# A transformer layer's modulation rows on six tiles, gates loaded a step ahead, and a staging tile in another pool

## The chip, the cores and the metric

The kernel runs on one core of a Trainium2 chip. The metric is device time in microseconds (us) of one execution. "Before" is the median of three runs: 2761.38 us (2759.38 to 2765.55). The profile is of one further execution.

Names of the engines in the profile: PE is TensorE (matrix products and transposes), PEld its weight load, DVE is VectorE, ACT is ScalarE, POOL is GpSimd, SP is SyncE, which here issues most of the transfers. Each engine takes its instructions in the order of its own queue. SPq and POOLq are the queues from which SyncE and GpSimd issue transfers.

## What is computed

One layer of a diffusion backbone on 256 latent tokens `x` and 256 context tokens `ctx`, width D = 2048, all in float32. Each sub-layer is normalised and modulated by rows of a product of a condition vector with `w_mod`; nine such rows (`N_MOD`) belong to each of the two sequences.

```python
def adaln(x, g, mod, i):
    return rms_norm(x, g) * (1 + mod[:, i + 1, None, :]) + mod[:, i, None, :]

def half_step_ffn(x, mod, i, g, w_up, w_down):
    h = adaln(x, g, mod, i)
    a, b = jnp.split(h @ w_up, 2, axis=-1)
    return x + 0.5 * mod[:, i + 2, None, :] * ((jax.nn.silu(a) * b) @ w_down)

def reference(...):
    mod_l = (silu_c @ w_mod[l] + b_mod[l]).reshape(B, N_MOD, D_MODEL)
    mod_c = (silu_cc @ w_mod[l] + b_mod[l]).reshape(1, N_MOD, D_MODEL)
    xl = half_step_ffn(xl, mod_l, 0, g_norm[l, 0], w_ffn1_up[l], w_ffn1_down[l])
    xc = half_step_ffn(xc, mod_c, 0, g_norm[l, 0], w_ffn1_up[l], w_ffn1_down[l])
    hl = adaln(xl, g_norm[l, 1], mod_l, 3)
    hc = adaln(xc, g_norm[l, 1], mod_c, 3)
    ...
    (aq_l, ak_l, av_l), m_l = mixer_projections(hl, *mix, rope)
    (aq_c, ak_c, av_c), m_c = mixer_projections(hc, *mix, None)
    hm_c, st_f, st_b = mlstm_bidir(*m_c[:3], *m_c[4:], zero_state, zero_state)
    hm_l, _, _ = mlstm_bidir(*m_l[:3], *m_l[4:], st_f, st_b)
    att_l = latent_attention(aq_l, ...)
    xl = xl + mod_l[:, 5, None, :] * mixer_output(att_l, hm_l, m_l[3], m_gain[l], w_out[l])
    xl = half_step_ffn(xl, mod_l, 6, g_norm[l, 2], w_ffn2_up[l], w_ffn2_down[l])
    return rms_norm(xl, g_final)
```

The mixer has 8 attention heads and 8 mLSTM heads of width 128. An mLSTM head takes query and key through a short convolution (5 taps) and Silu.

## The kernel before, in words

**Products.** A float32 weight tile of 128 x 2048 arrives in `raw` (three buffers) or `chain_` (two). `split` makes of each half `hi` (ScalarE, L102: a rounding copy) and `lo` (VectorE, L103: what the rounding left). `mm3` (L124 to L126) then multiplies three times: high by high, high by low, low by high. TensorE so needs both engines for each tile, `lo` last. `hi` and `lo` have four buffers each.

**Order of the stages.** FFN1's up projection runs in groups of products (`quad`), then its down projection in pairs of blocks (`pair`), a single last block (`last1`), the mixer's projections `w_c`, `w_a`, `w_b` (with gate algebra for the mLSTM, `gate_steps`), `w_mk` (eight heads), `w_mq` (eight heads), attention, `w_out`, and FFN2. By the matmuls of the profile `last1` begins near 1380 us, `w_c` 1427, `w_a` 1456, `w_b` 1492, `w_mk` 1540, `w_mq` 1645; attention and the heads' outputs go on to about 1892.

**Modulation beside the products.** One half-row block of `w_mod` (512 KB) is loaded into a tile `sraw` and multiplied by the broadcast condition `cBl` and summed by one VectorE instruction (`mod_half`, L183), pinned in program order. In the mixer `mod_late` hands 96 such items (rows 5 to 7) to `mod_items`, a generator stored in `beside["part"]`. `products_of` and `channels` take one step of it every few matmuls. `pace` maps items to steps: an item comes once `done` has reached the interpolated step. Two tiles serve all items: after each item the next but one is asked for into the tile that was just read, so SyncE's queue (L212) stands until VectorE has read it. `conditions` loads the other half of `cBl` when the items pass to the second half. `mod_end` finishes a row, `mod_rows_out` turns and stores it.

**Down projection.** `pair(p)` goes through seven products per pair of blocks, each for two column halves `c`. `chain_` is updated in place by accumulating transfers on GpSimd (`accum`). In the last pair the sums pass through the gate (`through_gate`, L853), and `both_gates` loads (L858) the gate rows of both sequences to 128 partitions (256 KB each) into a two-buffer tile `gate`, in the step that uses them. `last1` loads one gate half per column block in the same manner and writes through a one-buffer tile `y`.

**Hidden tiles.** FFN1's hidden state passes over HBM: `turned` transposes a tile, ScalarE copies it to `stg`, and SyncE stores it to `hidd` (profile: `hid<-stg`). `stg` lies in pool `f1u`. When that pool closes, pool `f1` with `acc` and the two-buffer tiles `two` (here named `v` and `gate`) takes its space. `last_steps` asks for two hidden tiles of the last block at step 8 of the last quad, on which two products of the first pair depend.

**mLSTM.** `conv` (L1175 on VectorE) and Silu lead to `mkT` and `mqT`. `state` (L1188, tile `vw`) makes the context's final state, two steps per head. `latents` loads `nM` for a head, multiplies key with query (L1241), makes the decay matrix `E` (L1250 on VectorE, L1252 and L1253 Exp on ScalarE, a mask on GpSimd), and `heads_out` ends with `hm` (L1293, L1294). Exp and Silu need different activation tables; ScalarE loads one at each change.

Pool `m1` holds most of this. `one(...)` makes a tile of one buffer; a `tag` names the slot it lives in, so that tiles with one tag share the space one after the other.

Of the kernel before, what the change touches and what calls it, by code (L numbers as in the profile page):

```python
# [18 lines left out]
P = 128  # L19
# [29 lines left out]
def tile_layer(ctx: ExitStack, tc: tile.TileContext, I: dict, out: bass.AP):  # L49
# [106 lines left out]
    class Conditions:  # L156


        def __init__(self, half, load, at):
            self.half, self.load, self.at = half, load, at  # L160
# [81 lines left out]
    def mod_late(sp, i0, i1, pace):  # L242

        cB = sp.tile([P, 1024], F32, name="cBl", bufs=1)
        cond = Conditions(lambda h: h, lambda h: conditions({LAT: cB}, h, h + 1, (LAT,)), lambda h: {LAT: cB})
        raws = lambda: sp.tile([P, 1024], F32, tag="sraw", name="sraw", bufs=2)
        return mod_items(half_items(i0, i1), nc.sync.dma_start, raws, 2, cond, None, pace)

    def mod_end(i, seqs):

# [322 lines left out]
    with pool(name="f1u", bufs=1) as f1u:  # L573
# [87 lines left out]
        def turned():  # L661

            if not turn:
                return
            n, t, ca = turn.pop(0)
            tb = tbank()
            for j in range(FB):
                nc.tensor.transpose(tb[:, j * P : (j + 1) * P], ca[:, j * P : (j + 1) * P], ident)
            stg = f1u.tile([P, CB], F32, tag="stg", name="stg")
            nc.scalar.activation(stg, tb, AF.Copy, scale=-1.0)  # L670
            nc.sync.dma_start(hidd[n][:, t].rearrange("p j c -> p (j c)"), stg)

# [102 lines left out]
        def last_steps(step):  # L775

            steps(side)
            if step == 8:
                raws.extend(hid_slot("n"))
                for m in range(2):  # L780
                    hid_load(m, raws[m].bitcast(F32))
            if step == 10:
                place0.extend(x.rearrange("p (a c) -> p a c", a=2) for x in hid_slot("s"))
            if step in (11, 12):
                split_to(place0[step - 11], quarters(raws[step - 11].bitcast(F32))[0])
# [69 lines left out]
    def both_gates(cb, seqs=(CTX, LAT)):  # L855
        g = two("gate")
        for s in seqs:
            nc.sync.dma_start(g[:, s, :], mod_rows[2][s, cb * CB : (cb + 1) * CB].partition_broadcast(P))  # L858
        return g

    NP = (NB - 1) // 2

    def pair(p):

        X, Y, Z, ra, gates = {}, {}, {}, {}, None
        w = lambda m, cb: I["w_dn1"][2 * p + m, cb]

        def put(t, cb, b, first=False):
            if first and p == 0:
                nc.scalar.activation(col(t, cb), b, AF.Copy)  # L870
            else:
                nc.vector.tensor_tensor(col(t, cb), col(t, cb), b, op=ALU.add)

        def through_gate(t, cb):

            if p < NP - 1:
                return
            s, tt = divmod(t, 2)
            half_gated(col(t, cb), col(t, cb), gates[:, s, :], -1.0 if cb % 2 else 1.0)
            accum(col(t, cb), xsrc[s][tt * P : (tt + 1) * P, cb * CB : (cb + 1) * CB])  # L880

        def c11x(c, s):
            put(2 * s, 2 * c, X[c, s], True)

        def c11z(c, s):
            put(2 * s, 2 * c, Z[c, s])
            through_gate(2 * s, 2 * c)

        def p5(c, s):
            put(2 * s + 1, 2 * c + 1, Y[c, s], True)  # L890

        def p35(c, s):
            put(2 * s, 2 * c + 1, Y[c, s], True)

        def c12(c, s):
            put(2 * s, 2 * c + 1, X[c, s])
            through_gate(2 * s, 2 * c + 1)

        def x3(c, s):
            put(2 * s + 1, 2 * c, X[c, s], True)  # L900
            put(2 * s + 1, 2 * c + 1, X[c, s])
            through_gate(2 * s + 1, 2 * c + 1)

        def c21(c, s):
            put(2 * s + 1, 2 * c, Y[c, s])
            through_gate(2 * s + 1, 2 * c)

        def loaded(m, cb):
            raw = raw_tile()
            nc.sync.dma_start(raw, w(m, cb))  # L910
            return raw

        def again(c):
            if p + 1 < NP:
                nc.sync.dma_start(chain_[c], I["w_dn1"][2 * p + 2, 2 * c])

        def b22(c):
            ra[c] = loaded(1, 2 * c + 1)
            return ra[c]

        held = lambda c: chain_[c]

        order = (
            ("a11", held, X, True, lambda c: accum(chain_[c], w(0, 2 * c + 1)), c11x, None),
            ("a12", lambda c: loaded(1, 2 * c), Z, True, None, c11z, 0),
            ("n1", held, Y, True, lambda c: accum(chain_[c], w(1, 2 * c + 1)), p5, None),
            ("s4", b22, Y, False, lambda c: accum(ra[c], w(0, 2 * c + 1)), p35, None),
            ("s2", held, X, False, lambda c: accum(chain_[c], w(1, 2 * c)), c12, 1),
            ("s3", lambda c: ra[c], X, False, None, x3, 1),
            ("a22", held, Y, True, again, c21, 0),  # L930
        )
        todo = first_plan if p == 0 else plan if p < NP - 1 else last_plan
        for m, (g, src, dst, fresh, then, use, gate) in enumerate(order):
            a = place0[m] if p == 0 and m < 2 else place[g]
            for c in range(2):
                wt = split(src(c))
                if then:
                    then(c)
                for x in todo.get(2 * m + c, "").split():
                    if x.startswith("raw"):  # L940
                        hid_load(2 * p + 2 + int(x[3]), raws[int(x[3])])
                    else:
                        make[x]()
                if p == NP - 1 and gate is not None:
                    gates = both_gates(2 * c + gate)
                for s in range(2):
                    if fresh:
                        dst[c, s] = tbank() if c and dst is not X else bank()
                    for j in range(FB):
                        k = slice((FB * s + j) * P, (FB * s + j + 1) * P)  # L950
                        mm3(dst[c, s], a[:, 0, k], a[:, 1, k], *wt(slice(j * CB, (j + 1) * CB)), fresh and j == 0, j == FB - 1, True)
                    use(c, s)
# [20 lines left out]
    def last1():  # L973

        norm = iter(())
        kept = {}
        for s in (CTX, LAT):
            for n, cb in enumerate((1, 3, 0, 2) if s == CTX else (2, 0, 3, 1)):
                c = slice(cb * CB, (cb + 1) * CB)
                wt = kept.pop(cb, None) or load_split(I["w_dn1"][NB - 1, cb])  # L980
                if s == CTX and n >= NCB - 2:
                    kept[cb] = wt
                g = both_gates(cb, (s,))[:, s, :]
                for t in range(2 * s, 2 * s + 2):
                    b = bank()
                    block_products(b, wt, t)
                    a = acc[:, t, c]
                    y = f1.tile([P, CB], F32, tag="xr", name="y", bufs=1)
                    half_gated(y, b, g)
                    nc.vector.tensor_tensor(a, a, y, op=ALU.add)  # L990
                    if s == LAT:
                        nc.sync.dma_start(x1d[(t - 2) * P : (t - 1) * P, c], a)
                    if n == 0:
                        ss1[t] = sm.tile([P, 4], F32, tag="ss4", name="ss4", bufs=4)
                    sumsq(ss1[t][:, cb : cb + 1], a)
                    steps(norm, (1, 0, 0, 0, 2, 2, 2, 2)[2 * n + t % 2])
            drain(norm)
            norm = adaln(s)
        return norm
# [32 lines left out]
    with ExitStack() as mx:  # L1032
# [21 lines left out]

        mmcm = pool(name="mm", bufs=1)

        beside["part"] = mod_late(mmcm.__enter__(), 5, 8, ((45, 44), (75, 96), (96, 160)))
        ev_mv(6, 0, b_c)
        b_a = {}
        drain(project("w_a", 416, range(4), b_a))  # L1060
# [13 lines left out]
        def gates():  # L1074
# [35 lines left out]
            for d in range(2):  # L1110
# [15 lines left out]
                nc.vector.tensor_tensor_scan(Mq, uq, uq, m3, ALU.max, ALU.max)  # L1126
                nc.vector.tensor_copy(hc[:, d, 4 + a : 5 + a], m2)
                nc.vector.tensor_tensor(hc[:, d, 4 + z : 5 + z], m2, btT[:, d, 2 + a : 3 + a], op=ALU.add)
            negM = one([NH, 2, T], "negM")
            nc.vector.tensor_scalar(negM, MT.rearrange("h d t q -> h d (t q)"), -1.0, None, op0=ALU.mult)  # L1130
            nc.sync.dma_start(negMd, negM)

# [26 lines left out]


        mkT = one([P, NH, T], "mkT")
        mqT = one([P, NH, T], "mqT")
        C1 = one([P, NH, 2, 130], "C1")

        def conv(b, ch, ns):
# [12 lines left out]
        def state(h, kTc):  # L1178
# [3 lines left out]
                nc.tensor.transpose(tb[:, t * P : (t + 1) * P], kTc[:, t * P : (t + 1) * P], ident)  # L1182
            kn = m1.tile([P, 2, P], F32, tag="kn", name="kn", bufs=1)
            nc.scalar.activation(kn, tb[:, :256].rearrange("p (t d) -> p t d", t=2), AF.Copy)
            vw = m1.tile([P, 2, 2, 130], F32, tag="vw", name="vw", bufs=1)
            for t in range(2):
                for d in range(2):
                    nc.vector.tensor_scalar(vw[:, t, d, :], v1[CTX][:, t, h, :], wg[:, t, d, h : h + 1], None, op0=ALU.mult)  # L1188
# [36 lines left out]
            todo.append((h, y))  # L1225


        hm = one([P, 2, 1024], "hm")
        ready = [0]

# [551 lines left out]
```

## Time and profile before

| what | us |
|---|---|
| median of the runs | 2761.38 |
| profiled execution | 2753.58 |
| its span | 2751.9 |
| TensorE clock granted over the span, of full | 0.986 |
| `L183` in the mixer: 96 instructions | 116.6 |
| `L103` lo, 128x1024, in 1440 to 1900: 76 instructions | 94.2 |

The profile gives busy times per engine, waits by engine, line and releaser (us in total, times, longest), and windows, which give each engine's busy time in a stretch with the granted clock and the transfer share. One group row reads: line, engine, operation, tiles out and in, number; busy time and mean in ns; idle time ahead of it and who ended it. For the modulation in the mixer, 1440 to 1900 us, that group is:

```profile
L183 DVE SCALAR_TENSOR_TENSOR sraw<-sraw,cBl 128x1024 f32<-128x1024 f32 x96 | 116.6, 1221 | 44.9 <-DMA sraw<-in_w_mt 42.0 <-DMA cBl<-ccd 2.4
```

The last figures say that VectorE stood idle for 44.9 us ahead of these 96 instructions, 42.0 of them until a row had landed. All 224 such loads of the kernel, of 512 KB each, take a median of 5.3 us from issue to landing:

```profile
sraw<-in_w_mt SPq DMA_DIRECT2D x224, 512.0 KB, 5.3
```

### The profile page before, as it was taken

Reading aid. Unit: us, or ns where it says so; the run is one execution under the profiler, and the core shown is the slowest. Engines: PE = TensorE matmul, PEld = TensorE weight load, DVE = VectorE, ACT = ScalarE, POOL = GpSimd, SP = SyncE. Lnnn points to the kernel's source line nnn. Section 1 sums busy time; section 2 is a strip of 40 time slices with the busy share of each in tenths; the row PEclk is TensorE's granted clock in tenths of the full one; section 3 lists DMA queues with packets and bytes.
Section 4 is the critical chain, followed back from the end, with each engine's and each line's share of the span. In section 5 each row is a group of like instructions: output and inputs, shape, how many; then the busy total and the mean of one; then the engine's idle time right before and its main releaser. Section 6 shows DMA issues by size and latency. Waiting matters only on the chain. (4 is left out here: it accounts for less than half of the span.)

```text
span 2751.9 us, 33080 instructions
## 1 busy us (share of the span) xinstructions
PE 2647.2 (96%) x12573; PEld 2180.0 (79%) x12573; DVE 1995.5 (73%) x2740; ACT 1263.4 (46%) x1586; POOL 174.6 (6%) x217
## 2 busy tenths in 40 slices
PE   6999999999999889999999998999999999999998
PEld 3588878887878768888789788877898888888886
DVE  2387778778877778888786789797685666666657
ACT  3454444544444455444363335345474444444444
POOL 0000000110000000000210000111000000000000
PEclk8999999999999999999999999999999999999999
DMA  8879999999999969889966766574466666666553
GB/s 349 313 233 249 246 274 277 263 269 268 269 254 266 269 193 239 224 233 219 227 220 217 257 236 234 178 259 161 163 230 227 216 228 223 217 225 225 211 190 132
DMA packets 125887, 645.32 MB, mean 235 GB/s; under 512 B 13464, under 2 KB 17560, under 8 KB 68256
## 3 DMA queue, kind: packets, MB, share of 16 engines
q1 hardware_dynamic: 106144, 513.18, 51.7%
q0 software_dynamic: 19584, 130.03, 24.1%
q8 instruction: 99, 1.62, 0.2%
q14 instruction: 60, 0.49, 0.0%
HBM read 627.36 MB, written 15.79 MB: 234 GB/s over the span
## 5 line engine op out<-in xcount | busy, mean ns | idle before, releaser
L103 DVE TENSOR_TENSOR lo<-raw,hi 128x1024 fp32r<-128x1024 f32 (+3 forms) x600 | 720.3, 1205 | 399.7 <-ACT hi L102 388.4
L102 ACT ACTIVATE hi<-raw 128x1024 fp32r<-128x1024 f32 (+3 forms) x600 | 625.2, 1045 | 796.4 <-PE mm L126 644.5
L125 PE MATMUL mm<-lo,hhi 128*128 128x512 f32 (+3 forms) x1024 | 392.5, 383 | 15.1 <-DVE lo L103 15.0
L124 PE MATMUL mm<-hi,hhi 128*128 128x512 f32 (+3 forms) x1024 | 394.2, 388 | 4.4 <-ACT v L1053 4.4
L126 PE MATMUL mm<-hi,hlo 128*128 128x512 f32 (+3 forms) x1024 | 391.0, 382 | 0.0
L102 ACT ACTIVATE hi<-chain 128x1024 fp32r<-128x1024 f32 x240 | 251.8, 1058 | 264.7 <-PE mm L126 129.5
L103 DVE TENSOR_TENSOR lo<-chain,hi 128x1024 fp32r<-128x1024 f32 x240 | 289.3, 1220 | 98.0 <-ACT hi L102 96.5
L183 DVE SCALAR_TENSOR_TENSOR c<-sraw,cBh 128x1024 bf16<-128x1024 f32 x192 | 229.3, 1218 | 36.8 <-DMA sraw<-in_w_mt 33.5
L124 PE MATMUL mm<-hi,h2hi 128*128 128x512 f32 x640 | 249.1, 389 | 0.0
L125 PE MATMUL mm<-lo,h2hi 128*128 128x512 f32 x640 | 249.0, 389 | 0.0
L126 PE MATMUL mm<-hi,h2lo 128*128 128x512 f32 x640 | 249.0, 389 | 0.0
L125 PEld LDWEIGHTS mm<-lo,hhi 128*128 128x128 f32 x1024 | 195.8, 191 | 51.3 <-DVE lo L103 19.8
L124 PEld LDWEIGHTS mm<-hi,hhi 128*128 128x128 f32 x1024 | 194.5, 190 | 36.6 <-ACT v L1053 4.8
L126 PEld LDWEIGHTS mm<-hi,hlo 128*128 128x128 f32 x1024 | 195.3, 191 | 34.0
L183 DVE SCALAR_TENSOR_TENSOR sraw<-sraw,cBl 128x1024 f32<-128x1024 f32 x128 | 155.6, 1220 | 44.9 <-DMA sraw<-in_w_mt 42.0
L124 PE MATMUL mm<-hhi,hi 128*128 128x512 f32 (+1 forms) x384 | 142.0, 371 | 1.2 <-ACT hi L102 1.2
L124 PEld LDWEIGHTS mm<-hi,h2hi 128*128 128x128 f32 x640 | 120.1, 188 | 25.2
L125 PEld LDWEIGHTS mm<-lo,h2hi 128*128 128x128 f32 x640 | 120.1, 188 | 24.8
L126 PEld LDWEIGHTS mm<-hi,h2lo 128*128 128x128 f32 x640 | 120.1, 188 | 24.8
L126 PE MATMUL mm<-hhi,lo 128*128 128x512 f32 (+1 forms) x384 | 137.9, 361 | 1.2 <-DVE lo L103 1.2
L124 PE MATMUL mm<-hi,hid2h 128*128 128x512 f32 x352 | 138.5, 395 | 0.0
L125 PE MATMUL mm<-hlo,hi 128*128 128x512 f32 (+1 forms) x384 | 138.4, 361 | 0.0
(377 smaller groups left out, 4719.3 us busy)
## 6 DMA issues: line engine op xcount, KB each, us to landing
sraw<-in_w_mt SPq DMA_DIRECT2D x224, 512.0 KB, 5.3
raw<-in_w_up2b SPq DMA_DIRECT2D x80, 1024.0 KB, 4.7
raw<-in_w_dn SPq DMA_DIRECT2D x70, 1024.0 KB, 4.8
chain<-in_w_up1b POOLq DMA_DIRECT2D x60, 1024.0 KB, 11.0
raw<-in_w_up1b SPq DMA_DIRECT2D x40, 1024.0 KB, 8.8
mraw<-in_w_m SPq DMA_DIRECT2D x32, 1024.0 KB, 8.0
chain<-in_w_dn POOLq DMA_DIRECT2D x30, 1024.0 KB, 9.3
chain<-in_w_up1b SPq DMA_DIRECT2D x20, 1024.0 KB, 7.1
```

The lines of the kernel that those rows point to most:

```text
L102: nc.scalar.activation(hi, src, AF.Copy)
L103: nc.vector.tensor_tensor(lo, src, hi.bitcast(F32), op=ALU.subtract)
L124: nc.tensor.matmul(out_ap, sh, mh, start=first, stop=False, skip_group_check=skip)
L125: nc.tensor.matmul(out_ap, sh, ml, start=False, stop=False, skip_group_check=skip)
L126: nc.tensor.matmul(out_ap, sl, mh, start=False, stop=last, skip_group_check=skip)
L183: ins = nc.vector.scalar_tensor_tensor(junk() if junk else raw, raw, 1.0, cB[s], op0=ALU.mult, op1=ALU.mult, accum_out=mT[:, i, s, kt, h : ...
```

## The change

Three things are changed.

*Modulation in the mixer.* The class `Beside` takes the place of `mod_late` there (FFN2 keeps the old one). It has six tiles: three `sr` of its own in pool `mm`, two halves of a tile in the slot of `mqT`, one in the slot of `rt`; both slots are used for their own tiles only later. The first six loads are issued by GpSimd, the others by SyncE. The next load into a tile is issued when one further step has passed since its use (`due`). The three borrowed tiles serve the first 50 items; `close_early` ends that before `mqT` is made, ahead of the w_mq heads. The pace is new. To make room, `negM` shares the slots `nM`, and `vw` the slots `E`, in place of slots of their own.

*Gates of the down projection.* In the last pair the table `GATES` says at which half-step which column block's gates are loaded; `ahead` holds those not used yet, and `s3` uses the gates that `s2` used. `last1` has a ring of four half tiles, each loaded two blocks ahead.

*Staging tile.* `stg` and `last1`'s `y` lie in pool `chp`, which lasts to the end of the down projection. The hidden tiles of the last block are asked for at step 6 of the last quad and not 8.

```diff
+    class Beside:
+        def __init__(self, sp, i0, i1, early, n_early, pace):
+            self.cB = sp.tile([P, 1024], F32, name="cBl", bufs=1)
+            self.items = half_items(i0, i1)
+            self.n_early, self.pace = n_early, pace
+            self.slots = {}
+            self.n = self.done = self.waits = self.asked = 0
+            self.due, self.late = [], []
+            for x in [sp.tile([P, 1024], F32, name=f"sr{j}", bufs=1) for j in range(3)]:
+                self.fetch(x, False, nc.gpsimd)
+            for x in early:
+                self.fetch(x, True, nc.gpsimd)
+
+        def fetch(self, x, early, queue):
+            if self.asked >= (self.n_early if early else len(self.items)):
+                return
+            i, kt, h = self.items[self.asked]
+            pin(queue.dma_start(x, I["w_mt"][i - 2, kt, :, h * 1024 : (h + 1) * 1024]))
+            self.slots[self.asked] = x, early
+            self.asked += 1
+
+        def one(self):
+            i, kt, h = self.items[self.n]
+            x, early = self.slots[self.n]
+            mod_half(x, {LAT: self.cB}, None, i, (LAT,), kt, h)
+            self.due.append((self.done + 1, self.n))
+            self.n += 1
+
+        def finish(self, n):
+            i, kt, h = self.items[n]
+            x, early = self.slots.pop(n)
+            self.fetch(x, early, nc.sync)
+            left[i] -= 1
+            if not left[i]:
+                self.late += [(self.done + 2, i, s, v) for s, v in mod_end(i, (LAT,))]
+
+        def close_early(self):
+            while self.n < self.n_early:
+                self.one()
+            while self.due:
+                self.finish(*self.due.pop(0)[1:])
+
+        def steps(self):
+            half = None
+            while self.n < len(self.items) or self.due or self.late:
+                while self.n < len(self.items):
+                    h = self.items[self.n][2]
+                    if h != half:
+                        half = h
+                        conditions({LAT: self.cB}, h, h + 1, (LAT,))
+                        self.waits += WAIT
+                    if self.done < np.interp(self.n, *zip((0, 0), *self.pace)) + self.waits:
+                        break
+                    self.one()
+                yield
+                self.done += 1
+                for x in [x for x in self.due if x[0] <= self.done]:
+                    self.due.remove(x)
+                    self.finish(*x[1:])
+                if self.late and self.late[0][0] <= self.done:
+                    mod_rows_out(*self.late.pop(0)[1:])
...
-            stg = f1u.tile([P, CB], F32, tag="stg", name="stg")
+            stg = chp.tile([P, CB], F32, tag="stg", name="stg")
...
-            if step == 8:
+            if step == 6:
                 raws.extend(hid_slot("n"))
...
+    LAST = [(CTX, cb) for cb in (1, 3, 0, 2)] + [(LAT, cb) for cb in (2, 0, 3, 1)]
+    last_gates = []
+
+    def last_gate(i):
+        if i % 4 in (0, 2) and len(last_gates) < 4:
+            g = two("gate")
+            last_gates.extend((g[:, 0, :], g[:, 1, :]))
+        if i < len(LAST):
+            s, cb = LAST[i]
+            nc.sync.dma_start(last_gates[i % 4], mod_rows[2][s, cb * CB : (cb + 1) * CB].partition_broadcast(P))
...
+        GATES = {0: 0, 1: 2, 4: 1, 5: 3, 11: 0, 12: 2}
+        ahead, used = [], {}
...
-                if p == NP - 1 and gate is not None:
-                    gates = both_gates(2 * c + gate)
+                if p == NP - 1:
+                    if (2 * m + c) in GATES:
+                        ahead.append(both_gates(GATES[2 * m + c]))
+                    if 2 * m + c == 13:
+                        last_gate(0)
+                        last_gate(1)
+                    if m in (1, 4, 6):
+                        gates = used[c] = ahead.pop(0)
+                    elif m == 5:
+                        gates = used[c]
...
-                g = both_gates(cb, (s,))[:, s, :]
+                last_gate(i + 2)
+                g = last_gates[i % 4]
...
-                    y = f1.tile([P, CB], F32, tag="xr", name="y", bufs=1)
+                    y = chp.tile([P, CB], F32, tag="stg", name="y")
...
-        beside["part"] = mod_late(mmcm.__enter__(), 5, 8, ((45, 44), (75, 96), (96, 160)))
+        early2 = one([P, 2, 1024], "early2", tag="mqT")
+        mods = Beside(mmcm.__enter__(), 5, 8, [early2[:, 0, :], early2[:, 1, :], one([P, 1024], "early1", tag="rt")], 50, ((6, 12), (50, 54), (70, 90), (84, 126), (96, 162)))
+        beside["part"] = mods.steps()
...
-            negM = one([NH, 2, T], "negM")
+            negM = m1.tile([NH, 2, T], F32, tag="nM", name="negM")
...
-        mqT = one([P, NH, T], "mqT")
...
-            vw = m1.tile([P, 2, 2, 130], F32, tag="vw", name="vw", bufs=1)
+            vw = m1.tile([P, 2, 2, 130], F32, tag="E", name="vw")
...
+        mods.close_early()
+        mqT = one([P, NH, T], "mqT")
```

More of the change, by code (lines that the diff above doesn't have):

```diff
@@ L249, in mod_end, with pin @@
+    def pin(ins):
+        tc.keep_in_program_order(ins)
     def mod_end(i, seqs):
@@ L859, in both_gates @@
         return g
+    LAST = [(CTX, cb) for cb in (1, 3, 0, 2)] + [(LAT, cb) for cb in (2, 0, 3, 1)]
[7 more added lines that the diff above has]
+            nc.sync.dma_start(last_gates[i % 4], mod_rows[2][s, cb * CB : (cb + 1) * CB].partition_broadcast(P))
     NP = (NB - 1) // 2
     def pair(p):
-        X, Y, Z, ra, gates = {}, {}, {}, {}, None
+        X, Y, Z, ra = {}, {}, {}, {}
+        gates = None
         w = lambda m, cb: I["w_dn1"][2 * p + m, cb]
@@ L921, in pair @@
         held = lambda c: chain_[c]
+        GATES = {0: 0, 1: 2, 4: 1, 5: 3, 11: 0, 12: 2}
+        ahead, used = [], {}
         order = (
[L924 to L930, printed above, removed]
+            ("a11", held, X, True, lambda c: accum(chain_[c], w(0, 2 * c + 1)), c11x),
+            ("a12", lambda c: loaded(1, 2 * c), Z, True, None, c11z),
+            ("n1", held, Y, True, lambda c: accum(chain_[c], w(1, 2 * c + 1)), p5),
+            ("s4", b22, Y, False, lambda c: accum(ra[c], w(0, 2 * c + 1)), p35),
+            ("s2", held, X, False, lambda c: accum(chain_[c], w(1, 2 * c)), c12),
+            ("s3", lambda c: ra[c], X, False, None, x3),
+            ("a22", held, Y, True, again, c21),
         )
         todo = first_plan if p == 0 else plan if p < NP - 1 else last_plan
-        for m, (g, src, dst, fresh, then, use, gate) in enumerate(order):
+        for m, (g, src, dst, fresh, then, use) in enumerate(order):
             a = place0[m] if p == 0 and m < 2 else place[g]
@@ L977, in last1 @@
         for s in (CTX, LAT):
-            for n, cb in enumerate((1, 3, 0, 2) if s == CTX else (2, 0, 3, 1)):
+            for i, (_, cb) in [(i, x) for i, x in enumerate(LAST) if x[0] == s]:
+                n = i % NCB
                 c = slice(cb * CB, (cb + 1) * CB)
```

## The prediction

> **What bounds the kernel now.** I read the busy times first, then TensorE's waits, then clock and load stage by stage, then the waits of the engines it waits for.
>
> ```profile
> PE 2647.2 (96%) x12573; PEld 2180.0 (79%) x12573; DVE 1995.5 (73%) x2740; ACT 1263.4 (46%) x1586; POOL 174.6 (6%) x217
> ```
>
> TensorE (PE) is busy for 2647.2 of a span of 2751.9 us. At most 104.7 us can be had without taking products away, plus what the clock loses. Its waits between 1440 and 1900 us, the mixer, are:
>
> ```profile
> PE tr L1285 <- DVE hm L1294: 6.8, 2, 4.8
> PE mm L1241 <- DVE mqT L1307: 4.7, 2, 3.9
> PE tr L1182 <- ACT cy L1224: 4.6, 2, 2.9
> PE mm L124 <- ACT v L1053: 4.4, 1, 4.4
> PE tr L1139 <- DVE hcd L1134: 2.4, 1, 2.4
> PE tr L1435 <- DVE pr L1429: 2.1, 1, 2.1
> ```
>
> With four small rows (1.4, 1.2, 0.5, 0.2) they add to 28.3 us. The windows around the longest gaps show a second loss (columns: length, busy time by engine, granted clock, DMA share, GB/s):
>
> ```profile
> 1498.00:1510.00 12.00, 11.98 (x56) 11.98 (x57) 6.81 (x13) 6.75 (x11) 0.00 (x0) 0.76 0.77 258
> 1530.00:1537.00 7.00, 6.89 (x34) 6.90 (x35) 5.01 (x13) 0.98 (x3) 0.00 (x0) 0.76 0.69 244
> 1565.00:1576.00 11.00, 10.35 (x33) 8.00 (x34) 10.34 (x19) 2.64 (x5) 0.00 (x0) 0.69 0.58 193
> 1660.00:1668.00 8.00, 6.62 (x33) 5.68 (x33) 6.37 (x17) 1.31 (x2) 0.00 (x0) 0.79 0.70 248
> 1718.00:1727.00 9.00, 8.49 (x35) 7.33 (x36) 9.00 (x30) 4.70 (x6) 0.00 (x0) 0.81 0.69 237
> 1848.00:1854.00 6.00, 5.67 (x23) 4.99 (x24) 5.41 (x12) 1.38 (x3) 0.65 (x1) 0.72 0.76 274
> ```
>
> Length times (1 - clock) is the time lost: 2.9, 1.7, 3.4, 1.7, 1.7 and 1.7, together 13.1 us. So the mixer holds 41.4 us to win. What holds VectorE (DVE) there, and SyncE's queue:
>
> ```profile
> DVE sraw L183 <- DMA sraw<-in_w_mt: 42.0, 28, 4.2
> DVE lo L103 <- ACT hi L102: 19.4, 11, 4.3
> SPq L212 <- DVE sraw L183: 181.2, 75, 7.6
> ```
>
> VectorE waits 28 times for a modulation row, since two tiles are loaded, used and only then loaded again. It takes its instructions in order, so `lo`, the convolution and the gate algebra stand behind those waits. Further waits lie outside the mixer, at the hand-over to FFN1's down projection (975 to 1016 us, first two rows) and in its last pair (1340 to 1376 us, third row):
>
> ```profile
> DVE v L820 <- DMA hid<-stg: 8.3, 1, 8.3
> ACT acc L870 <- DMA hid<-stg: 9.7, 1, 9.7
> DVE acc L853 <- DMA gate<-mod: 8.1, 2, 7.4
> ```
>
> **The change, part by part.** The profiled execution took 2753.58 us, 1.7 beyond its span and 7.8 below the median 2761.38. Terms are worked out on the former and taken off the median.
>
> *Staging tile.* `stg` moves out of a pool whose space the next stage's `acc` and `v` reuse. In the built order neither waits for the `hid<-stg` transfers any more, so rows of 9.7 and 8.3 us go from ScalarE and VectorE. What that is worth is PE's part: from 996 to 1013 us it waits 3.5 + 2.0 + 1.6 + 0.6 + 0.4 = 8.1 us, and the clock is 0.72 for 6 us (1.7). Next late is VectorE itself: the first four steps hold about 26 us of its instructions by their rows, and PE takes 21.8. Of that excess of 4 some 2.6 should stay as gaps, 0.7 as clock. I take -6.5, bounds 0 and -9.8. The hidden tiles of the last block, asked for at step 6 and not 8, move nothing: that stretch of SyncE's order is the same in both builds. Cost 0; the 6.1 us wait for `lo` at 960.7 stays.
>
> *Gates.* Twelve gate loads in the last pair in place of 16, each one step or more ahead, and a ring of four halves for the last block. Before, the load issued at 1346.25 landed at 1360.14; VectorE stood for it 7.4 us, and the `lo` behind it, whose `hi` was ready at 1359.5, started at 1360.84. PE's gaps are 3.3 + 2.9 = 6.2 us between 1360 and 1378, and 1.7 of clock behind the last (0.66 over 5 us). The weights come late too: the accumulating load issued at 1340.59 took 17.8 us with gate loads beside it. Dropping four of 256 KB is 1.0 MB less, 4.6 us at the 227 GB/s of the page's slice there (1307 to 1376). I take -6, bounds 0 and -7.9.
>
> *Modulation, early part (1440 to 1645).* All 96 half-rows stay on VectorE at 1220 + 81 ns: nothing added. Six tiles serve the first 50 and then three, a tile is asked for again a step after its use, and SyncE no longer stands at `L183`. Ahead of the gate algebra 10 `L183` stand and not 14; by the end of the w_b steps about 23 and not 30. So `v` (4.4), `hcd` (2.4) and `cy` (4.6) come earlier: 11.4 us and 2.9 + 1.7 + 3.4 = 8.0 of clock, 19.4 in all. The first loads are six on GpSimd's queue behind `tri_f`, `tri_b` and two memsets, which ended at 1455 us (0.88 us per issue, as for its chain loads), where SyncE sent two at 1427.6; before, the first `L183` ran at 1453.4. They land about 1462, and two `lo` are ahead of the first; the next is needed near 1469. The new pace asks for an item of 0.52 MB per 2.05 us step in w_b: 256 GB/s, with the weights 364. The fastest 50 us of the run move 378 (share 0.95), but w_b's own rate is 253 at share 0.76, or about 333 full. That is some 1 MB short over 33 us, two items, which six tiles mostly cover. I take -14, bounds 0 and -19.4.
>
> A rule of the Trainium skill bears on the clock part. "TensorE: Matmul & The Clock Gate", in the table of its section "Why this matters for your kernels", wants no PE-idle gap over about 3 us; shorter ones would cost only themselves. By that rule the reduced clock behind 1530 (1.7) and 1565 (3.4) isn't the gaps' doing and stays, and the forecast would be 5 us later, 2733. The trace speaks against it: gaps of 2.39 (1530) and 2.10 us (1848) were followed by a reduced clock, while 2.67 (1362) was not.
>
> *Modulation, late part (1645 to 1900).* The rest is hm 6.8, mqT 4.7, pr 2.1 and the four small rows 3.3, 16.9 us, and 5.1 of clock: 22. VectorE is what binds the mq steps:
>
> ```profile
> 1645.00:1678.00 33.00, 28.34 (x211) 27.08 (x211) 30.06 (x59) 11.67 (x17) 0.00 (x0) 0.95 0.69 236
> 1678.00:1711.00 33.00, 31.77 (x259) 30.86 (x258) 31.59 (x86) 25.51 (x36) 2.22 (x4) 1.00 0.71 240
> ```
>
> It is busy 61.7 of 66 us. In the built order, between the 37th and the 57th weight half (1652 to 1743.5 before) stand 18 `L183` and not 23; at the rows' durations this stretch holds 74.4 us of VectorE's work and not 82.4. Against that, `vw` and `negM` take tags that others hold, so the latent `E` work of the first two heads leaves 1541 to 1551, where VectorE waited for rows, and falls into these steps: 12 x 0.28 + 2 x 0.85 = 5.1 us (in the 74.4), and on ScalarE, at work for 37.2 of 66, six more table loads of 1.28 us, 7.7. I take -7. Bounds: -22, and above zero +8, all table loads on the path.
>
> Sum: -6.5 - 6 - 14 - 7 = -33.5. On the profiled time 2720, on the median **2728**; the parts' middling errors give 2714 to 2745.
>
> **The rivals.** A difference under 0.2%, 5.5 us, can't be told from none here.
>
> 1. *Transfers bind the modulation.* For it: 42.0 us of waits for rows, and 17 loads and more crowded into w_b. Against: share 0.69 to 0.77. The early part would then give a third, -5: sum -24.5, 2737.
> 2. *The two small edits give nothing*: VectorE's own 26 us replaces the staging wait, and the gate loads only queue elsewhere. For it: that excess, and landings of 12 to 18 us for every load there. Then -21, 2740.
> 3. *Slower: each mq head comes late.* Convolution, Silu, `mqT`, product L1241 is one chain per head. With the moved `E` work, ScalarE changes tables between Exp and Silu inside it. The wait at 1660.7 cost 3.9 + 1.7 = 5.6 us. If the six other heads without such a wait pay that, it is +33.6, and the late part's -7 is gone: -26.5 + 33.6 = +7, 2768. From five heads late on (28) it eats everything. For it: VectorE at 93%. Against: 8 us less on VectorE, and its rows are there in time.
> 4. *Nothing measurable*: two to four heads late, or early gains handed to the mq steps, about 2760.
>
> **Chances.** Forecast 0.44, rival 1 0.14, rival 2 0.12, rival 3 0.19, rival 4 0.07, and 0.04 for more than is forecast (the lower bounds add to -59, 2702). Faster is 0.44 + 0.14 + 0.12 + 0.04 = 0.74, same 0.07, slower 0.19. The range goes from 2706 to 2768: below lie 0.02, above about half of rival 3, so it holds some 0.88, which the parts' errors reduce to about 0.8. The likeliest case's own is 2714 to 2745.
>
> **What would show it.** No `hid<-stg` row for ScalarE and VectorE, and under 4 us of PE gaps from 996 to 1013. No `gate<-mod` row over 1 us in the last pair. `sraw`'s wait, now under the names of the six tiles, well under 42; rows of `v`, `hcd` and `cy` under 4 us together and granted clock 1.00 from 1492 to 1645. If waits for the new tiles are still over 25 us it is rival 1. If L1241 waits for `mqT` more often than twice, and VectorE is over 95% busy through the mq steps, it is rival 3. I am wrong at the root if PE's gaps shrink and the matmuls themselves become slower.

## The result and the profile after

The changed kernel took 2715.64 us, the median of four runs (2709.23 to 2716.65); the kernel before took 2763.05 beside it (2759.38 to 2765.55). The ratio is 0.9825, with a 95% interval from 0.9805 to 0.9844. That is 47.4 us less by the medians. The profiled execution took 2715.45 us, its span 2713.7, which is 38.2 less than the span before. The difference between 47.4 and 38.2 is a result of its own (below).

Line numbers have moved: L853 is now L923, L1182 is L1279, L1241 is L1340, L1285 is L1384, L1435 is L1534; `sraw` of the mixer is `sr` and `early`, and its later loads are issued at L271.

The page's first part:

```profile
PE 2635.2 (97%) x12573; PEld 2173.0 (80%) x12573; DVE 1993.7 (73%) x2740; ACT 1270.5 (47%) x1592; POOL 177.0 (7%) x223
```

The work is the same; the span around it is shorter. TensorE's waits in the mixer, 1425 to 1870 us (us in total, times, longest), which is the stretch shown of before:

```profile
PE mm L1340 <- DVE mqT L1406: 3.6, 1, 3.6
PE tr L1384 <- DVE kvs L1464: 1.9, 1, 1.9
PE mm L125 <- DVE lo L103: 1.8, 3, 0.9
PE tr L1279 <- ACT cy L1321: 1.7, 2, 1.2
PE tr L1534 <- DVE pr L1528: 1.5, 2, 1.3
```

The rows of `v`, `hcd` and `hm` (13.6 us together before) are gone, `cy` fell from 4.6 to 1.7. VectorE's waits in the same stretch:

```profile
DVE lo L103 <- ACT hi L102: 19.8, 10, 4.3
DVE lo L103 <- PE mm L1289: 10.8, 5, 3.8
...
DVE sr L183 <- DMA sr<-in_w_mt: 7.1, 2, 6.9
```

Waits for a modulation row fell from 42.0 us (28 times) to 7.1 (2 times), with 1.2 more for the borrowed tiles, and nearly all of that is one wait of 6.9. What VectorE waits for now is mostly `hi` and products, and no longer transfers. SyncE's queue still stands until `L183` has read a tile, for 107.1 us on the new tiles and 27.7 on the borrowed ones, together 134.8, where it stood 181.2 before. With more tiles the rows are there in time all the same. The load in the same stages (columns: length, busy time of PE, PEld, DVE, ACT, POOL, granted clock, DMA share, GB/s):

```profile
1505.00:1530.00 25.00, 25.00 (x132) 22.78 (x131) 24.41 (x53) 9.16 (x13) 0.00 (x0) 1.00 0.91 326
...
1616.90:1649.00 32.10, 28.47 (x214) 27.48 (x213) 31.05 (x66) 17.66 (x22) 1.70 (x4) 0.95 0.66 219
1649.00:1681.40 32.40, 31.35 (x256) 30.65 (x255) 31.39 (x85) 25.95 (x38) 2.16 (x4) 1.00 0.76 255
```

The first row is the end of w_b and the start of w_mk: transfers run at 326 GB/s, share 0.91, where they ran at 253 before, and TensorE has no gap. The other two are the mq steps: VectorE is busy for 62.4 of 64.5 us, fuller than before (61.7 of 66), and yet TensorE waits less.

At the hand-over, 985 to 1016 us, no row names `hid<-stg`, and one wait of TensorE is left:

```profile
PE mm L125 <- DVE lo L103: 0.3, 1, 0.3
```

In the last pair, 1330 to 1376 us, TensorE has no wait at all and VectorE's for gates are two short ones:

```profile
DVE y L923 <- DMA gate<-mod: 0.5, 1, 0.5
DVE acc L923 <- DMA gate<-mod: 0.3, 1, 0.3
```

Both traces hold 12573 matmuls, so the time between the same two of them can be compared. These differences to the kernel before, in us, are worked out so from the traces, of the changed kernel and of all experiments; stages are named by the times of before:

| | 380-975 | 975-1016 | 1355-1382 | 1382-1427 | 1492-1540 | 1540-1645 | 1645-1711 | 1711-1760 | 1760-1900 |
|---|---|---|---|---|---|---|---|---|---|
| changed | +11.2 | -10.9 | -8.7 | -1.0 | -11.3 | -6.6 | -1.6 | -5.6 | -2.5 |
| e1 | +8.0 | -10.8 | 0.0 | +0.5 | -0.6 | -1.9 | +0.1 | +1.2 | +0.8 |
| e2 | +1.5 | +0.1 | -7.8 | -1.0 | -2.1 | -0.1 | -0.4 | +0.5 | +0.2 |
| e3 | +5.7 | +0.3 | +0.3 | +2.9 | -11.3 | -7.0 | -1.8 | -5.6 | -1.7 |
| e4 | +15.8 | -10.8 | -8.2 | -1.0 | -10.9 | +3.1 | -1.6 | -5.6 | -2.4 |
| e5 | +15.0 | -10.8 | -8.7 | -1.0 | -11.3 | -7.0 | -1.4 | -3.4 | +0.2 |
| e6 | +11.1 | +1.6 | 0.0 | +1.9 | -9.3 | +2.7 | +1.9 | -5.6 | +0.6 |
| e7 | +12.0 | -10.4 | -8.7 | -1.0 | -11.3 | -6.9 | -1.6 | -5.6 | -2.5 |
| e8 | +9.2 | -10.8 | -1.2 | -1.0 | -11.3 | -7.2 | -2.2 | -5.6 | -1.7 |
| e9 | -4.8 | -10.8 | -7.5 | -1.0 | -8.3 | -6.2 | +2.4 | -5.9 | -2.2 |
| e10 | +8.7 | -10.8 | -8.7 | -1.0 | -9.2 | -4.8 | +3.9 | -6.6 | +0.4 |
| e11 | +11.3 | -10.8 | -8.7 | -1.0 | -11.3 | -7.4 | +4.4 | -4.0 | -1.4 |
| e12 | +5.4 | -0.4 | -8.4 | +2.2 | -1.0 | -0.3 | +1.8 | -0.4 | -0.1 |

Outside these columns the differences are 0.3 us or less, but for the first 380 us (up to 5.6). For the changed kernel, the stages that the change touches give -48.2 (-10.9 - 8.7 - 1.0 - 11.3 - 6.6 - 1.6 - 5.6 - 2.5), close to the 47.4 of the medians. The profile's 38.2 is smaller because FFN1's up projection (first column) took 11.2 us longer in this one execution.

### The profile page after: what moved, and what is told of

Read it like the earlier page. It is cut to its first block, busy times and chain, and to the rows that moved or that the text cites. A ratio compares the mean times of both kernels' runs of the same rounds, so it can differ in the third digit from the quotient of the medians.

```text
span 2713.7 us, 33046 instructions
## 1 busy us (share of the span) xinstructions
PE 2635.2 (97%) x12573; PEld 2173.0 (80%) x12573; DVE 1993.7 (73%) x2740; ACT 1270.5 (47%) x1592; POOL 177.0 (7%) x223
## 5 line engine op out<-in xcount | busy, mean ns | idle before, releaser
L183 DVE SCALAR_TENSOR_TENSOR c<-sraw,cBh 128x1024 bf16<-128x1024 f32 x192 | 229.6, 1220 | 43.0 <-DMA sraw<-in_w_mt 33.2
L126 PE MATMUL mm<-hi,hid2l 128*128 128x512 f32 x352 | 137.2, 390 | 0.0
## 6 DMA issues: line engine op xcount, KB each, us to landing
chain<-in_w_up1b POOLq DMA_DIRECT2D x60, 1024.0 KB, 11.1
```

Source lines behind the costliest of these rows:

```text
L126: nc.tensor.matmul(out_ap, sl, mh, start=False, stop=last, skip_group_check=skip)
L183: ins = nc.vector.scalar_tensor_tensor(junk() if junk else raw, raw, 1.0, cB[s], op0=ALU.mult, op1=ALU.mult, accum_out=mT[:, i, s, kt, h : ...
```

## The experiments

Each was timed in three rounds beside the kernel before; a ratio is to the kernel before, with its 95% interval. The runs of before ranged from 2749 to 2776 us, and the experiments are spread over four chips, so single microseconds are read from the stages in the table and not from the medians.

**e1, the staging tile alone.**

```diff
-            stg = f1u.tile([P, CB], F32, tag="stg", name="stg")
+            stg = chp.tile([P, CB], F32, tag="stg", name="stg")
...
-                    y = f1.tile([P, CB], F32, tag="xr", name="y", bufs=1)
+                    y = chp.tile([P, CB], F32, tag="stg", name="y")
```

> The kernel before with only the staging tile and y moved to the lasting pool. Theory: the hand-over's gain is the change's own and stands alone: from the matmul at 975 to that at 1016 us of the kernel before 10.9 us less, no wait of ScalarE or VectorE for hid<-stg, and a median 9 to 12 us below before (ratio about 0.996). Rival 1: VectorE's own excess of 4 us shows once the other parts are gone, the gain is 6 to 7 us. Rival 2: the 10.4 us that the changed kernel's profile loses between 400 and 975 us, in code that only the staging tile's place touches, are the price of that place; then this kernel loses them too and its median is within 2 us of before.

Measured: 2752.27 us against 2763.7, ratio 0.9957 (0.9939 to 0.9974), 11.4 us less. The hand-over is 10.8 us shorter, as with all parts. Rival 1 falls. The windows of before and after show where my excess went; before, from the matmul at 975 us:

```profile
975.00:997.60 22.60, 19.12 (x88) 15.44 (x87) 11.94 (x17) 9.79 (x15) 1.75 (x2) 1.00 0.73 192
997.60:1016.10 18.50, 13.80 (x47) 9.81 (x48) 17.42 (x18) 10.03 (x12) 1.58 (x2) 0.91 0.43 167
```

and after, over the same matmuls:

```profile
985.40:1004.30 18.90, 18.90 (x88) 15.63 (x88) 18.69 (x23) 14.15 (x19) 1.75 (x2) 1.00 0.75 184
1004.30:1015.70 11.40, 11.08 (x49) 8.72 (x48) 10.61 (x12) 6.24 (x7) 1.28 (x2) 1.00 0.89 322
```

VectorE (third busy time) has the same 29.4 and 29.3 us of work in both. Before, 11.9 of it was done in the first stretch, and after, 18.7: it starts in the time in which it had stood. That leaves 10.6 us for the second, where TensorE now needs 11.4.

Rival 2 falls too: it asked for a median within 2 us of before, and 11.4 us less were measured. The 8.0 us that this profile loses from 380 to 975 are no price of the new place that the medians would show. e2, e3, e6 and e12 have the code of before up to 975 us, and still took 1.5, 5.7, 11.1 and 5.4 us longer in that stretch: it differs between executions by itself, and the one profiled of before was the fastest of the five.

**e2, the gates alone** (the hunks on `GATES`, `ahead`, `last_gate`).

> The kernel before with only the gates loaded ahead (GATES and the ring of the last block). Theory: 8.7 us less from 1355 to 1382 us of the kernel before and 1.0 in the last block, median 8 to 11 us below before. Rival 1: the last pair's wait was a late echo of the staging wait, and alone the gates give under 4 us. Rival 2: the code up to 975 us is the same as before, and its profile there agrees with that of before to 1 us; if it differs by several us, that stretch differs from one execution to the next.

Measured: 2749.64 us against 2763.7, ratio 0.9957 (0.9936 to 0.9977), 14.1 us less by the medians. By stages 7.8 + 1.0 us. The theory holds by the stages, and rival 1, an echo of the staging wait with under 4 us, falls. The medians' 5 us more are within what these runs scatter.

**e3, the modulation alone** (class `Beside`, its use, the shared slots).

> The kernel before with only the modulation changed (six tiles, own pace, first loads by GpSimd, shared slots for negM and vw). Theory: 17.9 us less from 1440 to 1645 and 9.6 less from there to 1900, median 26 to 29 us below before. Rival: the parts help each other, since the changed kernel enters the mixer with its transfers less behind; then this part gives under 22 us and the three parts together less than the 47.4 us between the medians.

Measured: 2733.98 us against 2763.7, ratio 0.9905 (0.988 to 0.9931), 29.7 us less. By stages -11.3 - 7.0 - 1.8 - 5.6 - 1.7 = -27.4, against the changed kernel's -27.6. The parts don't help each other: e1, e2 and e3 give 10.8 + 8.8 + 27.4 = 47.0 us in the stages that they touch.

**e4, without the borrowed tiles.**

```diff
-            for x in early:
+            for x in early[:0]:
```

> The changed kernel without the three borrowed tiles: three tiles serve all 96 items, pace and all else as changed. If the depth of six gives the gain: the waits for rows come back (over 30 us of VectorE's time in the mixer), and the time is 10 us or more above the changed kernel. If the other parts of the edit give it (asking a step later instead of at the use, the pace): within 4 us of the changed kernel.

Measured: 2725.66 us, ratio 0.9882 (0.985 to 0.9914), 10 us above the changed kernel's median. VectorE's wait for rows is back in part (1440 to 1900 us):

```profile
DVE sr L183 <- DMA sr<-in_w_mt: 25.2, 14, 6.8
```

The loss is in one stage: w_mk is 3.1 us longer than before where six tiles make it 6.6 shorter, 9.7 in all. In w_b three tiles do nearly as well as six.

**e5, the old pace on six tiles.**

```diff
-..., 50, ((6, 12), (50, 54), (70, 90), (84, 126), (96, 162)))
+..., 50, ((45, 44), (75, 96), (96, 160)))
```

> The changed kernel with the old pace (45 items by step 44, 75 by 96, 96 by 160) on the six tiles. If the pace matters: 14 and not 10 items ahead of the gate algebra, so the waits for v and hcd come back, 5 us or more above the changed kernel. If the tiles alone matter: within 3 us of it.

Measured: 2725.09 us, ratio 0.9873 (0.9847 to 0.9899). The reason I gave is wrong: the w_b stage keeps all of its 11.3 us, with 16 items ahead of the gate algebra (10 in the changed kernel's trace, 14 before). What is lost is 4.9 us after 1711 (-3.2 against -8.1), where `hm` and `pr` are waited for again (1660 to 1900 us):

```profile
PE tr L1384 <- DVE hm L1393: 4.6, 2, 2.6
PE tr L1534 <- DVE pr L1528: 2.8, 1, 2.8
```

**e6, the new pace on the two tiles of before.**

```diff
-... mod_late(mmcm.__enter__(), 5, 8, ((45, 44), (75, 96), (96, 160)))
+... mod_late(mmcm.__enter__(), 5, 8, ((6, 12), (50, 54), (70, 90), (84, 126), (96, 162)))
```

> The kernel before with the new pace alone, on its two tiles asked for at the use. If the pace alone gives the gain: 15 us or more below before. If the tiles give it: within 5 us of before, since VectorE still waits some 40 us for rows.

Measured: 2753.15 us against 2761.08, ratio 0.9965 (0.9945 to 0.9984). Neither answer was right. VectorE still waits for rows (1440 to 1900 us),

```profile
DVE sraw L183 <- DMA sraw<-in_w_mt: 30.5, 27, 3.4
```

and w_mk and the mq steps lose 4.6 us together; but w_b gains 9.3 and the stretch from 1711 to 1760 5.6. With e5 this says: in w_b either fewer items ahead of the gate algebra or tiles that are there in time gives most of the gain (with the pace alone TensorE still waits 2.0 us for `hcd`). From 1711 to 1760 the pace alone gives all of the 5.6 us, the tiles alone 3.4. From 1760 on neither gives anything alone (+0.6, +0.2); together they give 2.5.

**e7, the first loads on SyncE.**

```diff
-                self.fetch(x, False, nc.gpsimd)
+                self.fetch(x, False, nc.sync)
...
-                self.fetch(x, True, nc.gpsimd)
+                self.fetch(x, True, nc.sync)
```

> The changed kernel with its first six row loads issued by SyncE, in front of the second w_a tile, and not by GpSimd. My prediction held GpSimd's late start (1455 us) as nearly free. If so: within 2 us of the changed kernel. If the start on GpSimd costs, this is 2 to 5 us faster. If six loads on SyncE's queue hold the weights back, it is 2 to 8 us slower, with new gaps of TensorE in w_a or w_b.

Measured: 2713.52 us, ratio 0.9826 (0.9796 to 0.9855); no stage of the mixer differs from the changed kernel's by more than 0.3. The queue of the first loads doesn't matter.

**e8, sixteen gate loads, all ahead.**

```diff
-        GATES = {0: 0, 1: 2, 4: 1, 5: 3, 11: 0, 12: 2}
+        GATES = {0: 0, 1: 2, 4: 1, 5: 3, 9: 1, 10: 3, 11: 0, 12: 2}
...
-                    if m in (1, 4, 6):
-                        gates = used[c] = ahead.pop(0)
-                    elif m == 5:
-                        gates = used[c]
+                    if m in (1, 4, 5, 6):
+                        gates = ahead.pop(0)
```

> The changed kernel, but with s3 loading its gates again, a step ahead as the others: 16 gate loads in the last pair as before, and only earlier. My prediction gave part of the gain to the 1.0 MB that is not loaded (4.6 us earlier weights) and part to the earlier issue. If the early issue alone gives it: the stretch that was 1355 to 1382 us in the kernel before stays 8.7 us shorter. If the traffic does: 3 us or more of it come back.

Measured: 2726.06 us, ratio 0.9871 (0.9837 to 0.9905). Of the last pair's 8.7 us, 1.2 are left. VectorE waits for gates from 1330 to 1380 us as in the kernel before (8.6 there, 7.4 at the longest):

```profile
DVE acc L923 <- DMA gate<-mod: 9.5, 3, 8.0
```

Earliness in the program gave nothing, because the tile that the second load of a gate needs is only free when `s2` has used it: the first was issued at 1347.65 us here and at 1346.25 before, and landed 14.5 and 13.9 us later.

**e12, only the reuse.** This run takes the kernel before and drops the second load alone.

```diff
-            ("s3", lambda c: ra[c], X, False, None, x3, 1),
+            ("s3", lambda c: ra[c], X, False, None, x3, None),
...
-                    gates = both_gates(2 * c + gate)
+                    gates = used[c] = both_gates(2 * c + gate)
+                elif p == NP - 1 and m == 5:
+                    gates = used[c]
```

> The kernel before with one edit: s3 uses the gates that s2 loaded, so 12 gate loads in the last pair and not 16; every other load stays in the step that uses it. The run with 16 loads ahead won only 1.2 us of 8.7 from 1355 to 1382, with an 8.0 us wait of VectorE for a gate. If that wait for the reload is what cost the time: this stretch is 7 to 8.7 us shorter here with nothing loaded ahead, and the last block is unchanged. If loading ahead and fewer loads are both needed: under 5 us.

Measured: 2755.5 us against 2763.81, ratio 0.9966 (0.9949 to 0.9982); the last pair is 8.4 us shorter. From 1330 to 1390 us VectorE's only row of a wait for gates is one of the last block:

```profile
DVE y L853 <- DMA gate<-mod: 0.6, 1, 0.6
```

Nearly all of the gates' gain is that `s3` doesn't ask again for what `s2` still holds. It isn't traffic on the weights: the last accumulating load took 17.4 us after the change, 17.8 before, and 17.85 here. The last block, expected unchanged, took 2.2 us longer from 1382 to 1427; in e3 and e6, which have the code of before there too, it took 2.9 and 1.9.

**e9 and e10, five tiles, with shared slots and with slots of their own.** The two were made as a pair, with one own tile fewer, to make room:

```diff
-            for x in [sp.tile(..., name=f"sr{j}", bufs=1) for j in range(3)]:
+            for x in [sp.tile(..., name=f"sr{j}", bufs=1) for j in range(2)]:
```

and in e10 also

```diff
-            negM = m1.tile([NH, 2, T], F32, tag="nM", name="negM")
+            negM = one([NH, 2, T], "negM")
...
-            vw = m1.tile([P, 2, 2, 130], F32, tag="E", name="vw")
+            vw = m1.tile([P, 2, 2, 130], F32, tag="vw", name="vw", bufs=1)
```

> The changed kernel with two tiles of its own and three borrowed, so five for the first 50 items and two after. Made to be compared with the next run. By itself: with the depth worth 9.7 us between six and three tiles in w_mk, five should lose 0 to 3 us there, and from two tiles in the mq steps VectorE should wait for rows again, 3 to 10 us lost after 1645.

> The same five tiles, with negM and vw in slots of their own as in the kernel before, so that the latent E work of the first heads can run ahead of the mq steps again. My prediction put the price of sharing at up to 7.7 us of table loads on ScalarE. If sharing costs: this is 3 to 8 us below the run before it, in the stretch from 1592 to 1711 us of the kernel before. If it is free: within 1 us of it in every stretch from 1440 on.

Measured: 2723.49 and 2723.77 us, ratios 0.9865 (0.9828 to 0.9903) and 0.9865 (0.9823 to 0.9907). From 1492 to 1900 e9 is at -8.3 - 6.2 + 2.4 - 5.9 - 2.2 = -20.2 and e10 at -16.3: own slots are 0.9 and 0.7 us faster in two stages (1492 to 1540, 1711 to 1760), and 3.9 slower in all, which neither answer had. The third own tile, the sixth in all, is worth 27.6 - 20.2 = 7.4 us. Own slots did what they were for: the `E` work of the first two heads (its masks on GpSimd) began at 1608 to 1619 us by the times of before, and at 1655 to 1672 in e9. ScalarE's table loads hardly went with it: 27 in e9, 25 in e10, 19 in the kernel before over the same matmuls (1440 to 1900). With five tiles, sharing had no price that shows.

**e11, four items put off at the turn to w_mq.**

```diff
-... ((6, 12), (50, 54), (70, 90), (84, 126), (96, 162))
+... ((6, 12), (50, 54), (51, 69), (70, 92), (84, 126), (96, 162))
```

> The changed kernel with a pace that puts off four items around the turn from w_mk to w_mq (item 51 at step 69, item 70 at step 92). There TensorE still waits 3.6 us for the first mqT, with two L183 in the chain ahead of it, and loses 1.7 us of clock after it. If those two L183 hold the chain up: the wait falls under 2 us, no reduced clock follows, and the stretch from 1592 to 1711 is 3 to 5 us shorter than in the changed kernel. If the chain is held up by the E work and the convolutions themselves: no change there, and the items put off cost up to 3 us later.

Measured: 2719.32 us, ratio 0.985 (0.9815 to 0.9885); the stretch from 1645 to 1711 is 6.0 us worse than in the changed kernel. The wait that it was to shorten is still there (1625 to 1900 us), and one of 1.7 us for `hm` comes beside it:

```profile
PE mm L1340 <- DVE mqT L1406: 3.9, 1, 3.9
```

The chain is held by more than those items. No run beat the changed kernel clearly: e7's median is 2.1 us lower, with intervals that overlap.

## Why the prediction was right, and where its sizes were off

The direction, the three places and the waits that go were right, and 2715.6 us lies in the range of 2706 to 2768. The forecast of 2728 is 12 us too high, and the result lies at the low edge of the likeliest case's 2714 to 2745. All four terms came out larger than forecast, the first two beyond their own bounds, and the reason given for the last one does not hold. By terms:

| term | forecast | measured, same matmuls |
|---|---|---|
| staging tile | -6.5 (0 to -9.8) | -10.9 |
| gates | -6 (0 to -7.9) | -9.7 |
| modulation to 1645 | -14 (0 to -19.4) | -17.9 |
| modulation from 1645 | -7 (+8 to -22) | -9.7 |
| sum | -33.5 | -48.2 |

*Staging tile.* The step that failed is "Of that excess of 4 some 2.6 should stay as gaps". I held 26 us of VectorE's work against 21.8 of TensorE's from the moment at which the transfer used to land. Without the wait VectorE starts earlier; the two windows under e1 show 6.8 us of it done ahead. A gap of 0.3 was left. The gain is 1.1 us more than the 9.8 of gaps and clock that were its bound, and the runs don't explain this rest. Rival 2 falls with e1 and e2: the two small edits give 10.8 and 8.8 us.

*Gates.* The wait of 7.4 us was the cause, as the prediction put it. "The weights come late too" gave part of the gain to 1.0 MB less traffic; e8 and e12 show that it is the second load of a gate still held. The measured gain of the pair is 0.8 over gaps plus clock (6.2 + 1.7), which the runs don't explain. The 1.0 us of the last block comes with the ring of gates, since every run that has the ring is at -1.0 there and those without are at 0.5 to 2.9.

*Modulation, early part.* `v` and `hcd` no longer wait, `cy` only 1.7 us, the clock is full from 974 to 1633 us of the changed kernel's trace, and transfers ran at 326 GB/s. Rival 1 needed waits of over 25 us for the new tiles; 8.3 were measured (7.1 + 1.2). With three tiles its sign would have come (e4: 25.2). The term kept 5 us back for a shortfall of two rows that six tiles covered. One premise failed without harm: "SyncE no longer stands at `L183`", where its queue still stood 134.8 us. The Trainium skill's rule against which the clock part was weighed ("TensorE: Matmul & The Clock Gate", section "Why this matters for your kernels") would have left the reduced clock behind 1530 and 1565 in place. It is gone with the gaps, which were of 2.4 and 2.9 us.

*Modulation, late part.* The step that failed is the 8 us less of VectorE's work, "74.4 us of VectorE's work and not 82.4" with "18 `L183` and not 23". The first window goes from the `lo` at 1652.2 to the one at 1743.5 us before, the second, of the changed kernel, between the same two:

```profile
1652.20:1743.50 91.30, 80.64 (x533) 74.13 (x533) 82.69 (x207) 47.90 (x65) 4.21 (x8) 0.96 0.69 238
1623.30:1710.70 87.40, 81.98 (x551) 75.64 (x550) 82.70 (x210) 53.20 (x73) 6.17 (x12) 0.98 0.71 239
```

VectorE works for 82.7 us in both, with 20 `L183` before and 19 after. What went is standing: in this stretch it waited 4.3 us for rows before and not at all after, and the stretch is 3.9 us shorter. So in this stretch the gain isn't that of a relieved VectorE, and the first argument against rival 3 was wrong as well.

The term's cost was over-sized: ScalarE's table loads rose by six as forecast, from 19 to 25, but e9 against e10 finds none of the up to 8 us set for them and the shared slots. From 1711 on the gain is of the pace and the tiles in the shares that e5 and e6 show. Rival 3's sign, VectorE over 95% busy, came true at 97%, but `mqT` was waited for once and not more than twice. A full engine isn't by itself late. That it is where its items stand that counts is suggested by e5 and e6, and not shown for the mq heads: there e11 put items off and lost 6.0 us.

*Against the profiled execution.* I took terms off the median and not off the profiled time. That was right, since the profiled execution of before was 7.8 us faster than the median, and four further traces with the same code took 1.5 to 11.1 us longer from 380 to 975.

## What to carry to other kernels

When a wait goes, let the engine that waited start earlier before you look for what is late next: its work then lies in the time in which it stood, and a residue worked out from the old landing time is too large. Before you load something ahead, ask whether it has to be loaded at all; a second load into a held buffer can't be issued before that buffer is free, however early it stands in the program. And compare two kernels over the same matmuls, stage by stage: here this told a gain of 1 us from scatter of 10.

## What the runs showed of the hardware

The clock is reduced on a grid, not by the length of a gap. In all 14 traces the reduced stretches begin and end on a grid with a step of 3.413 us (but for the end of the last one, which is the trace's), and a step at 0.50 follows a step in which TensorE stood for more than about half. Worked out from the traces, among steps at full clock from 100 to 2700 us of each span: of 100 in which TensorE had no matmul for 55% or more (1.9 us), 99 were followed by a reduced one; of 26 with 50 to 55%, 8; of 49 with 40 to 50%, 2; of 140 with 23 to 40%, none. The edge isn't sharper than that: near 70 us three steps idle for 55% were not followed by one either. So the 2.67 us gap of before that ends at 1362, split by the grid, cost only itself, and the one of 2.10 that ends at 1848 cost 1.7 us more (half of a step). In the changed kernel the gap of 3.6 us ahead of the first `mqT` brings a reduced step, and the one of 1.9 us at 1746, split by the grid, doesn't:

```profile
1632.00:1640.00 8.00, 7.63 (x40) 7.01 (x41) 7.46 (x22) 1.65 (x3) 0.00 (x0) 0.79 0.53 189
1742.00:1750.00 8.00, 6.12 (x34) 4.90 (x33) 7.50 (x23) 3.67 (x7) 1.70 (x2) 1.00 0.68 256
```

Second, the stretch from 380 to 975 us differs between executions: the five traces with the code of before there lie 11.1 us apart, and the nine with the changed staging tile 20.6 (-4.8 to +15.8). What makes it differ wasn't tried.
